# Reloading the context outputs of a first attention on another gate, and a margin in the plan ahead of the feed-forward's norm matmuls

## The chip, the cores and the metric

The kernel runs on one core of a Trainium2 chip. A core has a matrix engine (TensorE, PE in the profile, with its weight loads shown apart as PEld), a vector engine (VectorE, DVE), a scalar engine (ScalarE, ACT), GpSimd (POOL) and the engine that issues the transfers (SyncE, SP). Each works through its own list of instructions in a fixed order and waits for the others by semaphores. The metric is the device time of one execution in microseconds (us); what is given for a kernel is the median of several executions.

## The reference

A trunk of two layers over 1024 latent tokens and 256 context tokens, width 1024, 16 heads of 64. Layer 0 uses neighbourhood attention, layer 1 sliding-window attention; each layer ends with a gated feed-forward with a short convolution. The part that the change touches is the end of layer 0's attention and the start of its feed-forward:

```python
q, k, v = attn_inputs(h, w_in, gq, gk, n_kv)
q_c, k_c, v_c = attn_inputs(hc, w_in, gq, gk, n_kv, with_q=not last)
o = neighbourhood_attention(q, k, v, k_c, v_c, na_rpb[j])
x = x + gt1 * (o @ w_out)
o_c = attend(q_c, k_c, v_c, sink=sink).reshape(bsz, n_ctx, D_MODEL)
ctx = ctx + gt1c * (o_c @ w_out)
h = modulate(rmsnorm(x, g_ffn[i]), sh2, sc2)
x = x + gt2 * conv_ffn(h, ffn_w_up[i], ffn_conv_w[i], ffn_conv_b[i], ffn_w_down[i])
hc = modulate(rmsnorm(ctx, g_ffn[i]), sh2c, sc2c)
ctx = ctx + gt2c * conv_ffn(hc, ffn_w_up[i], ffn_conv_w[i], ffn_conv_b[i], ffn_w_down[i])
```

All of it is float32. The kernel makes a product of two float32 matrices out of three matrix multiplications of a reduced type: every operand is split into a high part and a low part, and hi·hi, lo·hi and hi·lo are added in PSUM. A split costs one ScalarE copy (the high part) and one subtraction on VectorE or GpSimd (the low part).

## The kernel before

Nothing in the program text fixes the order of the work. Each stage is described as operations with an engine, an estimated duration, tokens that are read and written, a key (a smaller key goes first among those that are ready) and places in rings of buffers; `class Sched` (L61) simulates the engines with these estimates and so settles the order in which each engine's instructions are issued. A wrapper records them, and so every row of the profile names L51, the wrapper's line; tiles are told apart by their names.

Layer 0's attention runs over 8 head pairs (0 to 7). For each, ten token tiles (8 of latents, numbers 8 and 9 of context) get their q, k and v by matmuls into `mm` tiles (`mm<-whi,h0hi` and the like); `s` are the scores, `S` the softmax tiles on VectorE and ScalarE, `pt` the transposes, `pthi`, `ptlo` the split probabilities, `pv` the products with v, and `osb` the output of a unit. The outputs of head pairs 0 to 6 are stored to `o_dram`; those of pair 7 stay on chip and are split directly.

Then comes the output projection, of class `Oproj` (L722), made as `op0` at L962 with three gates, lists of tokens on which operations wait. `gate` is the set of the qkv accumulations of all ten token tiles of head pair 7; `c_gate` is only those of the context tiles 8 and 9; `w_gate` is that of tile 4. Its methods:

- `weights` (L751) loads one 128x1024 slice of the output weights into a `woraw` tile of the ring `raw` (3 buffers), and splits it into `whi` (ScalarE) and `wlo` (GpSimd or VectorE in this stage, as the plan picks), in the ring `w` (4 pairs).
- `split` (L737) splits loaded attention outputs; for the context (`c == 2`) it waits on `c_gate`, for the latents on `gate`.
- `project` (L769) makes the matmuls of one output slice, waiting on `gate`.

`plan_oproj0` (L1184) plans the context part and the loads of the latent part. Two transfers bring the context outputs of head pairs 0 to 3 and 4 to 6 back as `craw` tiles (also in `raw`); they are split into `o2chi` and `o2clo`. Eight output slices (dt 0 to 7) follow, each 24 matmuls `mm<-o2chi,whi`, `mm<-o2clo,whi`, `mm<-o2chi,wlo` of 128x256, 192 in all. `evac` (L1197) loads the residual of a slice from `in_xseq_dram` into a `cx` tile (ring `qraw`, 2 buffers), adds the projected slice times its gate on VectorE and stores the sum to `c_dram`. The latent outputs come back as `oraw` tiles and are split into `o0hi`, `o0lo`, `o1hi`, `o1lo`.

All operations of this stage have keys from `OKEY` = 1000 up, so that the attention's operations go first where both are ready.

`ffn` (L1246) then plans the rest: the latent part of the output projection (`oacc<-o0hi,whi` and the like, 128x512; residual additions into `x` tiles), and, in `plan_ctx` (L1462), the context's norm. There `xc` is loaded from `c_dram`, `plan_sums` (L1289) squares it on ScalarE and adds the eight squares into `nsum` on VectorE, and `plan_bc` (L1313) sums over partitions on TensorE (`mp<-invd,nsum`), takes the root on VectorE and GpSimd (`n1v`, `n1y`, `n1t`) and broadcasts it (`bc`). A parameter `late` of `plan_bc` stands in the plan as an operation of its own engine, which does nothing on the chip, between the sums and the `mp` matmuls: the plan takes the sums to be there by so much later.

Of the kernel before, what the change touches and what calls it, by code (L numbers as in the profile page):

```python
# [19 lines left out]
KT = 8  # L20
# [16 lines left out]
WBUFS = 4  # L37
# [189 lines left out]
def trunk_kernel(ctx, tc, xperm, xseq, cc, wmod, bmod, gnorm, na_wqkv, na_gq, na_gk, na_bias, na_wo,  # L227
# [3 lines left out]
    act, dve, pool, pe, dma = [InOrder(tc, e) for e in (nc.scalar, nc.vector, nc.gpsimd, nc.tensor, nc.sync)]  # L231
# [103 lines left out]
    def t_dve(n):  # L335
        return 0.065 + n / 960.0
# [453 lines left out]
    with tc.tile_pool(name="x0", bufs=1, reuse_waits="tile") as xp, \  # L790
# [10 lines left out]
        for c, parts, key in ((2, 2, 0), (0, 4, 2), (1, 4, 30)):  # L801
            t0, n = CH[c]
# [21 lines left out]
        for v in range(2):  # L824
            J = {}
# [97 lines left out]
        for j in range(4):  # L923
# [5 lines left out]
                  key=50 + 2 * j, acq=[("w", ("w", j), 1)], rel=[("raw", j)])  # L929
            sa.op("dve", 0.87, lambda e, j=j: slabs.lo(j, e), reads=[("raw", j), ("wh", j)] + [("modc", 1)] * (j > 0),  # L930
                  writes=[("wl", j)], key=50 + 2 * j, rel=[("raw", j)])
# [25 lines left out]
    def pair(a):  # L957
# [3 lines left out]
    sc = Sched(dict(CAPS, klt=1))  # L961
    op0 = Oproj(sc, 0, 2, TC, psa, [("q0", HP - 1, tt, "acc") for tt in range(NT)],  # L962
                [("q0", HP - 1, tt, "acc") for tt in (8, 9)], [("q0", HP - 1, WG0, "acc")])
    OKEY = 1000
# [219 lines left out]
    def plan_oproj0():  # L1184
        C = {}
        for j, (a, b) in enumerate(((0, 4), (4, 7))):
            def load(e, j=j, a=a, b=b):
                C[j] = rpool.tile([P, 4, TC], F32, tag="raw", name="craw")
                dma.dma_start(C[j][:, :b - a], o_dram[0][a:b, :, T:].rearrange("k p t -> p k t"))
            sc.op("dma", 1.8, load, reads=[("od", k, 4) for k in range(a, b)] + op0.gate, writes=[("craw", j)], key=OKEY + j,  # L1190
                  acq=[("raw", ("craw", j), 2)])
            op0.split(2, (2, "j", j), 256 * (b - a), lambda j=j, n=b - a: C[j][:, :n], lambda x, a=a, b=b: x[:, a:b, :],
                      OKEY + j, [("craw", j)], [("craw", j)])
        parts = [[(x, 2, "j", int(k > 3)) for x in ("oh", "ol")] for k in range(7)] + [[(x, 2, 7) for x in ("oh", "ol")]]
        xin = {}

        def evac(dt, I):  # L1197
            def load(e):
                xin[dt] = wk.tile([P, 384], F32, tag="qraw", name="cx", bufs=2)
                dma.dma_start(xin[dt][:, :TC], xseq[:, KT * T + dt * TC:KT * T + (dt + 1) * TC])  # L1200
            xk = ("cx", dt)
            sc.op("dma", 0.6, load, reads=[("q0", HP - 1, ORDER[-1], "raw")], writes=[xk], key=OKEY + dt, acq=[("qraw", xk, 1)])

            def add(e):
                dve.scalar_tensor_tensor(out=xin[dt][:, :TC], in0=op0.acc[dt][:, :TC], scalar=modc[:, 0, 1, 2, dt:dt + 1],
                                         in1=xin[dt][:, :TC], op0=ALU.mult, op1=ALU.add)
            sc.op("dve", t_dve(TC), add, reads=[I, ("modc", 2), xk], writes=[xk], key=OKEY + dt, rel=[I], port=False)
            sc.op("dma", 0.6, lambda e: dma.dma_start(c_dram[:, dt * TC:(dt + 1) * TC], xin[dt][:, :TC]), reads=[xk],
                  writes=[("cd", dt)], key=OKEY + dt, rel=[xk])

        for dt in range(KT + NPRE):
            op0.weights(dt, na_wo[dt % KT], OKEY + dt, KT, [("craw", 0), ("craw", 1)] if dt >= WBUFS else ())
            if dt < KT:
                op0.project(dt, OKEY + dt, parts, evac)
        R = {}
        for kt in range(HP - 1):
            def load(e, kt=kt):
                R[kt] = rpool.tile([P, T], F32, tag="raw", name="oraw")
                dma.dma_start(R[kt], o_dram[0][kt, :, :T])
            r = ("oraw", kt)  # L1220
            sc.op("dma", 1.8, load, reads=[("od", kt, su) for su in range(4)] + op0.gate, writes=[r], key=OKEY + 0.5 + kt,
                  acq=[("raw", r, 4)])
            for c in range(2):
                op0.split(c, (c, kt), 512, lambda c=c, kt=kt: R[kt].rearrange("p (k r c) -> p r k c", k=8, r=16)[:, 8 * c:8 * c + 8],
                          lambda a, kt=kt: a[:, kt, :].rearrange("p (r k c) -> p r k c", r=8, k=8), OKEY + 0.5 + kt, [r], [r])
# [20 lines left out]
    def ffn(l, opj, xt1, todo):  # L1246
# [8 lines left out]
        sc = Sched(dict(b=8, raw=3, w=WBUFS, x=8, sr=SRB, g=GB, g2=GB, sq=2), {"b", "raw", "w", "x", "sr", "g", "g2", "sq"})  # L1255
# [57 lines left out]
        def plan_bc(nm, n, J, key, late=0.0):  # L1313

            I = (f"nm{nm}",)
            nt = n // P

            def mp(e):
                J["mp"] = bank("mp")
                for i in range(nt):  # L1320
                    pe.matmul(J["mp"][:, i:i + 1], J["t"][:, i * P:(i + 1) * P], invd, start=True, stop=True)

            sc.op(f"late{nm}", late, lambda e: None, reads=[I + ("sums",)], writes=[I + ("here",)], key=key)
            sc.op("pe", 0.11 * 2 * nt, mp, reads=[I + ("sums",), I + ("here",)], writes=[I + ("mp",)], key=key, acq=[("b", I + ("mp",), 1)])

            def v(e):
                for s in "vyt":
                    J["n" + s] = tiny.tile([P, 4], F32, tag="n1" + s, name="n1" + s, bufs=1)[:, :nt]
                dve.tensor_scalar(out=J["nv"], in0=J["mp"][:, :nt], scalar1=EPS, scalar2=None, op0=ALU.add)
            sc.op("dve", 0.07, v, reads=[I + ("mp",)], writes=[I + ("v",)], key=key, rel=[I + ("mp",)])  # L1330
            sc.op("pool", 0.96, lambda e: pool.tensor_tensor(out=J["ny"], in0=J["nv"], in1=mhalf[:, :nt], op=ALU.pow),
                  reads=[I + ("v",)], writes=[I + ("y",)], key=key)

            def newton(e):
                y, t, v = J["ny"], J["nt"], J["nv"]
                dve.tensor_tensor(out=t, in0=y, in1=y, op=ALU.mult)
                dve.scalar_tensor_tensor(out=t, in0=t, scalar=-0.5, in1=v, op0=ALU.mult, op1=ALU.mult)
                dve.scalar_tensor_tensor(out=y, in0=t, scalar=1.5, in1=y, op0=ALU.add, op1=ALU.mult)
            sc.op("dve", 0.473, newton, reads=[I + ("y",)], writes=[I + ("y",)], key=key)

            def dg(e):
                for i in range(nt):
                    dve.tensor_scalar(out=J["t"][:, 512 + i * P:512 + (i + 1) * P], in0=idf, scalar1=J["ny"][:, i:i + 1],
                                      scalar2=None, op0=ALU.mult)
            sc.op("dve", 0.15 * nt, dg, reads=[I + ("y",)], writes=[I + ("dg",)], key=key)

            def bc(e):
                J["bp"] = bank("bc")
                for i in range(nt):
                    pe.matmul(J["bp"][:, i * P:(i + 1) * P], ones, J["t"][:, 512 + i * P:512 + (i + 1) * P], start=True, stop=True)  # L1350
            sc.op("pe", 0.22 * nt, bc, reads=[I + ("dg",)], writes=[I + ("bp",)], key=key, acq=[("b", I + ("bp",), 1)])

            def bs(e):
                J["bc"] = J["t"][:, :n]
                act.activation(J["bc"], J["bp"][:, :n], AF.Copy)
            sc.op("act", t_actp(n), bs, reads=[I + ("bp",), I + ("mp",)], writes=[I + ("bc",)], key=key,
                  rel=[I + ("bp",), I])
# [104 lines left out]
        def plan_ctx():  # L1462
            n = TC
# [6 lines left out]
                dma.dma_start(Xc[0], c_dram.rearrange("p (k t) -> p k t", k=KT))  # L1470
            sc.op("dma", 3.6, load, writes=[("xc", k) for k in range(KT)], key=-30)
            J = plan_sums("c", n, xc, ct, lambda k: -20)
            plan_bc("c", n, J, -20)
            hc = []
            csh, csc = [modc[:, l, 1, v, :] for v in (3, 4)]
            for k in range(KT):
# [10 lines left out]
            for ft in range(FT):  # L1487
                key = KC + 8.7 * ft
                st = {}
                I = ("uc", ft)  # L1490
                for part in range(2):
                    W = cw(("cw", ft, part), w_up[l, ft + part * FT], key - 16 + 3 * part, 4)
                    for k0 in range(0, KT, 2):
                        def mm(e, part=part, k0=k0, W=W, st=st):
# [3 lines left out]
                            for k in (k0, k0 + 1):  # L1498
# [6 lines left out]
                              writes=[I, ("hcu",)], key=key + 3 * part, acq=[("b", I, 6)] if part == 0 and k0 == 0 else (), rel=[t])  # L1505
# [11 lines left out]
                for part in range(2):  # L1517
                    w = cv[:, l, ft + part * FT, :]
                    for tap, d in ((0, -1), (2, 1)):
# [8 lines left out]
                      reads=[g + (1,)], writes=[g + (0,)], key=key)  # L1528

                def ghi(e, st=st, ft=ft):  # L1530
# [4 lines left out]
                      reads=[g + (0,), g + ("h",)], writes=[g + ("l",)], key=key, rel=[("gt", ft)])  # L1535
                t = ("cd", ft)
                W = cw(t, w_down[l, ft], key - 8, KT)
                for dt in range(KT):
                    def mm(e, ft=ft, dt=dt, W=W):
# [4 lines left out]
                        for i, (w, b) in enumerate(((0, 0), (0, 1), (1, 0))):  # L1544
# [3 lines left out]
                          key=key + 13, acq=[("b", ("dnc", dt // 2), 2)] if ft == 0 and dt % 2 == 0 else (), rel=[t, g])  # L1548
            key = KU + 5
            for j in range(2):  # L1550
# [7 lines left out]
                for dt in range(4 * j, 4 * j + 4):  # L1558
                    def ev(e, dt=dt, R=R):
# [5 lines left out]
                      writes=[("c2", j)], key=key, rel=[r])  # L1565
# [20 lines left out]
        def t34_(i):  # L1586
            if not t34:
# [3 lines left out]
              writes=[("dsh",)], key=-50)  # L1591
        rx = lambda c, k, n=1: [("xt", c, k // 2)] * n if c or not last else []
        kb = 46.0 * n_todo
        for k in range(KT):
            key = 46.0 * (1 if not last else 0) + k
# [17 lines left out]
        for step in range(3):  # L1613
            for j in range(4):
                key = kb + (30.0 * j + 4 * step if not last else 2.0 * j + 8 * step)
                sh = shift[:, j + 4:j + 5]
                if step == 0:
# [3 lines left out]
                        writes=[("x", 0, j)], key=key)  # L1621
# [6 lines left out]
                else:  # L1628
                    sc.op("dve", tst, stt(1, j, 1, j + 4, dsh[:, j:j + 1], 1, j), reads=[("x", 1, j + 4), ("dsh",)],
                          writes=[("x", 1, j)], key=key, rel=rx(1, j + 4))  # L1630
# [8 lines left out]
        for j in range(4):  # L1639
            key = kb + (30.0 * j + 12 if not last else 2.0 * j + 24)  # L1640
            k = j + 4
# [472 lines left out]
    sc = Sched(CAPS)  # L2114
# [351 lines left out]
```

## Time and profile before

| What | Value |
|---|---|
| Median of 3 runs | 2849.25 us (2848.09 to 2849.77) |
| Profiled execution, its own time | 2851.74 us |
| Span of the profiled execution | 2850.0 us |
| Mean granted TensorE clock | 0.989 |
| VectorE busy | 2324.1 us (82%) |
| Transfers | 367.20 MB, 129 GB/s in the mean |

The span is cut into stages of quite different limits; the first attention ends near 720 us. Views by windows give the busy time of each engine in a stretch, in the order PE, PEld, DVE, ACT, POOL, then the granted clock (1.00 is full speed), the busy share of the transfer engines and GB/s. In a timeline, the brackets at the end of a row give the idle time of the engine ahead of it and what ended that. A matmul's duration in a row includes its way through the pipeline, so that successive rows overlap.

### The profile page before, as it was taken

Reading aid. Unit: us, or ns where it says so; the run is one execution under the profiler, and the core shown is the slowest. Engines: PE = TensorE matmul, PEld = TensorE weight load, DVE = VectorE, ACT = ScalarE, POOL = GpSimd, SP = SyncE. Lnnn points to the kernel's source line nnn. Section 1 sums busy time; section 2 is a strip of 40 time slices with the busy share of each in tenths; the row PEclk is TensorE's granted clock in tenths of the full one; section 3 lists DMA queues with packets and bytes.
Section 4 is the critical chain, followed back from the end, with each engine's and each line's share of the span. In section 5 each row is a group of like instructions: output and inputs, shape, how many; then the busy total and the mean of one; then the engine's idle time right before and its main releaser. Section 6 shows DMA issues by size and latency. Waiting matters only on the chain.

```text
span 2850.0 us, 46124 instructions
## 1 busy us (share of the span) xinstructions
PE 2784.4 (98%) x16344; PEld 2455.3 (86%) x16344; DVE 2324.1 (82%) x5243; ACT 1713.2 (60%) x3382; POOL 400.1 (14%) x675
## 2 busy tenths in 40 slices
PE   6999999999999999999999999999999999999999
PEld 5999999998789987777788888999987788888887
DVE  7888888888688687877797787999987988888757
ACT  5877777778456554444454457888873554455443
POOL 1222212223000000000010006455520000000000
PEclk9999999999999999999999999999999999999999
DMA  6222222314745544444375551010234323324745
GB/s 247 65 95 80 83 67 75 96 60 125 250 142 192 183 162 140 154 142 160 135 258 194 181 169 29 13 34 16 73 128 138 116 105 111 111 93 149 253 148 182
DMA packets 140953, 367.20 MB, mean 129 GB/s; under 512 B 21425, under 2 KB 34225, under 8 KB 139313
## 3 DMA queue, kind: packets, MB, share of 16 engines
q1 hardware_dynamic: 140720, 364.25, 38.1%
q8 instruction: 129, 2.11, 0.3%
q14 instruction: 104, 0.84, 0.1%
HBM read 297.21 MB, written 66.98 MB: 128 GB/s over the span
## 4 chain that ended last, share of the span: by engine, by line
PE 69%; DVE 4%; ACT 2%; issue 1%; DMA 1%; DVEq 0%; ACTq 0%; SPq 0%
PE ua L51 17%; PE dn L51 15%; PE uc L51 13%; PE mm L51 6%; PE oacc L51 4%; PE ud L51 4%; PE pt L51 3%; PE pv L51 2%; PE dnc L51 2%; PE s L51 2%; DVE S L51 1%; PE mod L51 1%; ACT S L51 1%; DVE ptlo L51 1%; DVE x L51 0%
## 5 line engine op out<-in xcount | busy, mean ns | idle before, releaser
L51 ACT ACTIVATE whi<-wraw 128x512 fp32r<-128x512 f32 (+1 forms) x264 | 212.6, 806 | 203.6 <-PE uc L51 62.7
L51 DVE TENSOR_TENSOR wlo<-wraw,whi 128x512 fp32r<-128x512 f32 (+1 forms) x264 | 239.2, 907 | 45.3 <-ACT whi L51 44.8
L51 DVE TENSOR_TENSOR ptlo<-pt,pthi 128x512 fp32r<-128x512 f32 (+2 forms) x384 | 223.2, 595 | 48.6 <-ACT pthi L51 45.0
L51 PE MATMUL dn<-ghi,wlo 128*128 128x512 f32 x616 | 242.4, 394 | 0.0
L51 PE MATMUL dn<-ghi,whi 128*128 128x512 f32 x616 | 242.4, 394 | 0.0
L51 PE MATMUL dn<-glo,whi 128*128 128x512 f32 x616 | 242.3, 393 | 0.0
L51 ACT ACTIVATE pthi<-pt 128x512 fp32r<-128x512 f32 (+2 forms) x384 | 195.1, 524 | 71.1 <-PE pt L51 61.1
L51 ACT ACTIVATE S<-S,m 128x640 f32<-128x640 f32 (+3 forms) x288 | 220.8, 768 | 22.7 <-DVE m L51 19.6
L51 DVE SCALAR_TENSOR_TENSOR u<-c,cv,u 128x1023 f32<-128x1023 f32 x176 | 223.2, 1279 | 6.8 <-ACT u L51 5.8
L51 ACT ACTIVATE whi<-s 128x1024 fp32r<-128x1024 f32 (+1 forms) x120 | 113.3, 945 | 191.4 <-PE uc L51 137.4
L51 ACT ACTIVATE ghi<-graw 128x512 fp32r<-128x512 f32 x154 | 96.4, 631 | 190.2 <-PE dn L51 108.4
L51 PE MATMUL pt<-idr,S 128*128 128x128 f32 x1280 | 199.2, 278 | 6.8 <-DVE sm L51 2.6
L51 PE MATMUL mm<-whi,h0hi 128*128 128x384 f32 x512 | 181.1, 354 | 0.4 <-ACT qraw L51 0.4
L51 DVE TENSOR_TENSOR glo<-graw,ghi 128x512 fp32r<-128x512 f32 x154 | 105.4, 688 | 83.8 <-ACT ghi L51 76.4
L51 PE MATMUL mm<-wlo,h0hi 128*128 128x384 f32 x512 | 172.3, 337 | 0.0
L51 PEld LDWEIGHTS pt<-idr,S 128*128 128x128 f32 x1280 | 153.5, 143 | 17.4 <-DVE ptlo L51 3.9
L51 DVE TENSOR_TENSOR wlo<-s,whi 128x1024 fp32r<-128x1024 f32 (+1 forms) x120 | 129.6, 1080 | 40.6 <-ACT whi L51 40.5
L51 POOL TENSOR_TENSOR qy<-qv,mhalf 128x4 f32<-128x4 f32 (+2 forms) x120 | 126.2, 1052 | 227.0 <-DVE qv L51 197.0
L51 PE MATMUL pv<-ptlo,v 128*128 128x256 f32 (+1 forms) x688 | 153.9, 297 | 1.2 <-DVE ptlo L51 1.2
L51 PE MATMUL pv<-pthi,v 128*128 128x256 f32 (+1 forms) x688 | 147.7, 287 | 4.1 <-DVE osb L51 3.0
L51 PE MATMUL ua<-t12hi,whi 128*128 128x512 f32 x352 | 138.7, 394 | 5.5 <-ACT t12hi L51 3.9
L51 POOL TENSOR_TENSOR n1y<-n1v,mhalf 128x4 f32<-128x4 f32 (+1 forms) x9 | 9.2, 1025 | 953.3 <-DVE n1v L51 950.7
(315 smaller groups left out, 8906.4 us busy)
## 6 DMA issues: line engine op xcount, KB each, us to landing
wraw<-in_w_up_dram SPq DMA_DIRECT2D x132, 512.0 KB, 3.4
wm<-in_wmod_dram SPq DMA_DIRECT2D x80, 512.0 KB, 4.0
wraw<-in_w_down_dram SPq DMA_DIRECT2D x44, 512.0 KB, 3.5
graw<-g_dram SPq DMA_DIRECT2D x44, 512.0 KB, 4.4
wraw<-in_w_down_dram SPq DMA_DIRECT2D x88, 256.0 KB, 3.0
graw<-g_dram SPq DMA_DIRECT2D x66, 256.0 KB, 2.8
slab<-in_na_wqkv_dram SPq DMA_DIRECT2D x32, 384.0 KB, 3.7
woraw<-in_na_wo_dram SPq DMA_DIRECT2D x24, 512.0 KB, 4.4
```

Source lines behind the costliest of these rows:

```text
L51: r = f(*a, **k)
```

## The change

```diff
-            sc.op("dma", 1.8, load, reads=[("od", k, 4) for k in range(a, b)] + op0.gate, writes=[("craw", j)], key=OKEY + j,
+            sc.op("dma", 1.8, load, reads=[("od", k, 4) for k in range(a, b)] + op0.c_gate, writes=[("craw", j)], key=1000 + j,
                   acq=[("raw", ("craw", j), 2)])
             op0.split(2, (2, "j", j), 256 * (b - a), lambda j=j, n=b - a: C[j][:, :n], lambda x, a=a, b=b: x[:, a:b, :],
-                      OKEY + j, [("craw", j)], [("craw", j)])
+                      1000 + j, [("craw", j)], [("craw", j)])
...
         for dt in range(KT + NPRE):
-            op0.weights(dt, na_wo[dt % KT], OKEY + dt, KT, [("craw", 0), ("craw", 1)] if dt >= WBUFS else ())
+            op0.weights(dt, na_wo[dt % KT], 1000 + dt if dt < 4 else OKEY + dt, KT, [("craw", 0), ("craw", 1)] if dt >= WBUFS else ())
...
             J = plan_sums("c", n, xc, ct, lambda k: -20)
-            plan_bc("c", n, J, -20)
+            plan_bc("c", n, J, -20, 5.0)
```

Two edits have an effect. The load of the two `craw` tiles waits for the context tiles' accumulations of head pair 7 instead of for all ten tiles'. And the plan takes the context norm's sums to be ready 5.0 us later than before. Since `OKEY` is 1000, the keys written as 1000 are the same numbers as before. No operation is added or taken away; the plan gives another order.

On SP, whose list of transfers is in one order for all, the `craw` loads stood between the loads of the output weights, the residuals and the latent outputs:

```order
L51 DMA woraw<-in_na_wo_dram 128x1024
L51 DMA craw<-o_dram_75 128x4x256
L51 DMA cx<-in_xseq_dram 128x256
L51 DMA oraw<-o_dram_75 128x1024
L51 DMA craw<-o_dram_75 128x3x256
L51 DMA cx<-in_xseq_dram 128x256
```

Now both stand next to each other, further ahead in the list, within head pair 7:

```order
L51 DMA o_dram_75<-osb 128x256
L51 DMA craw<-o_dram_75 128x4x256
L51 DMA craw<-o_dram_75 128x3x256
L51 DMA bias<-in_na_bias_dram 128x640
L51 DMA o_dram_75<-osb 128x256
```

They moved ahead of every load of output weights; a load of position bias and an output store stand behind them.

On TensorE, at the end of the attention, the first context projection matmul stood behind the transposes of the first softmax tile after the last qkv matmuls (`kkc`, `klc`, `kkl`, `kll` are the keys' high and low parts, `st` and `idr` the operands of the transposes):

```order
L51 MATMUL pv<-pthi,v 128x256 x2
L51 MATMUL pt<-idr,st 128x128 x4
L51 MATMUL pv<-ptlo,v 128x256 x2
L51 MATMUL pv<-pthi,v 128x256 x2
L51 MATMUL pv<-ptlo,v 128x256 x2
L51 MATMUL pt<-idr,S 128x128
L51 MATMUL s<-kkc,q 128x256
L51 MATMUL s<-klc,q 128x256
```

The same place now:

```order
L51 MATMUL pv<-pthi,v 128x256 x2
L51 MATMUL mm<-o2chi,whi 128x256
L51 MATMUL mm<-o2clo,whi 128x256
L51 MATMUL mm<-o2chi,wlo 128x256
L51 MATMUL mm<-o2chi,whi 128x256
L51 MATMUL mm<-o2clo,whi 128x256
L51 MATMUL mm<-o2chi,wlo 128x256
L51 MATMUL mm<-o2chi,whi 128x256
L51 MATMUL mm<-o2clo,whi 128x256
L51 MATMUL mm<-o2chi,wlo 128x256
L51 MATMUL mm<-o2chi,whi 128x256
L51 MATMUL mm<-o2clo,whi 128x256
```

Twelve context projection matmuls went ahead of `pt<-idr,st`; six more follow `pt<-idr,S`, 27 the `s` and `pv` of the next rows, and so on. Behind the attention's last `pv` there are 36 of the 192 left, where there were 78. The other matmuls of this stretch are the same in number.

On TensorE, around the `mp` matmuls of the context norm, before (the number at the end of a name tells the tiles of one name apart):

```order
L51 MATMUL oacc_11137<-o0hi0_10374,whi_11079 128x512
L51 MATMUL oacc_11137<-o0lo0_10378,whi_11079 128x512
L51 MATMUL oacc_11137<-o0hi0_10374,wlo_11080 128x512
L51 MATMUL mp_11194<-invd_93,nsum_11141 128x1 x2
L51 MATMUL oacc_11198<-o0hi0_10374,whi_11086 128x512
L51 MATMUL oacc_11198<-o0lo0_10375,whi_11086 128x512
```

and now:

```order
L51 MATMUL oacc_11194<-o0hi0_10349,whi_11084 128x512
L51 MATMUL oacc_11194<-o0lo0_10353,whi_11084 128x512
L51 MATMUL oacc_11194<-o0hi0_10349,wlo_11085 128x512
L51 MATMUL mp_11230<-invd_93,nsum_11141 128x1 x2
L51 MATMUL oacc_11194<-o0hi0_10349,whi_11084 128x512
L51 MATMUL oacc_11194<-o0lo0_10353,whi_11084 128x512
L51 MATMUL oacc_11194<-o0hi0_10349,wlo_11085 128x512
L51 MATMUL oacc_11239<-o0hi0_10349,whi_11208 128x512
L51 MATMUL oacc_11239<-o0lo0_10350,whi_11208 128x512
L51 MATMUL oacc_11239<-o0hi0_10349,wlo_11209 128x512
```

Before, 48 `oacc` matmuls stood ahead of `mp` and the first one behind it began a new output slice; now 69 stand ahead, and three matmuls behind `mp` a slice begins with weights `whi_11208` and `wlo_11209`, of which `wlo_11209` is first used in the sixth matmul behind `mp`. From the norm's broadcast on, TensorE's order is the same in both.

VectorE's rows there follow suit. Before:

```order
L51 TENSOR_TENSOR nsum<-nsum,sq 128x256 x5
L51 TENSOR_SCALAR x_11127<-oacc,modc,x_11127 128x512
L51 TENSOR_SCALAR n1v<-mp 128x2
L51 TENSOR_TENSOR nsum<-nsum,sq 128x512
L51 TENSOR_TENSOR n1t<-n1y 128x2
```

and now:

```order
L51 TENSOR_TENSOR nsum<-nsum,sq 128x256 x5
L51 TENSOR_SCALAR x_11127<-oacc,modc,x_11127 128x512
L51 TENSOR_TENSOR nsum<-nsum,sq 128x512
L51 TENSOR_TENSOR wlo<-woraw,whi 128x1024 x2
L51 TENSOR_SCALAR n1v<-mp 128x2
L51 TENSOR_SCALAR x_11135<-oacc,modc,x_11135 128x512
```

Two weight splits moved from behind the norm's short operations to between the last sum and `n1v`.

## The prediction, made before the changed kernel ran

> **What bounds the kernel now.** I read first the page's busy shares, then busy time by windows around the end of the first attention (600 to 750 us), then TensorE's timeline there, then the chain of waits.
>
> ```profile
> PE 2784.4 (98%) x16344; PEld 2455.3 (86%) x16344; DVE 2324.1 (82%) x5243; ACT 1713.2 (60%) x3382; POOL 400.1 (14%) x675
> ...
> core 0: us, PE busy (x) PEld busy (x) DVE busy (x) ACT busy (x) POOL busy (x), PEclk, DMA share, GB/s
> 600.00:640.00 40.00, 40.00 (x296) 39.65 (x295) 32.12 (x114) 29.05 (x77) 7.43 (x11) 1.00 0.16 50
> 665.00:679.00 14.00, 8.91 (x53) 7.29 (x53) 13.76 (x43) 13.28 (x32) 6.92 (x7) 0.82 0.53 159
> 679.00:690.00 11.00, 11.00 (x76) 11.00 (x76) 8.12 (x23) 6.73 (x16) 4.95 (x5) 0.76 0.47 148
> 690.00:700.00 10.00, 9.07 (x76) 8.78 (x75) 9.60 (x28) 6.98 (x19) 3.61 (x3) 1.00 0.34 110
> 700.00:710.00 10.00, 10.00 (x85) 9.89 (x85) 9.41 (x29) 9.90 (x22) 1.29 (x1) 1.00 0.65 198
> 710.00:720.00 10.00, 9.06 (x75) 8.69 (x75) 8.89 (x15) 5.57 (x12) 1.33 (x1) 1.00 0.66 209
> 730.00:740.00 10.00, 7.04 (x32) 5.49 (x30) 4.45 (x9) 3.83 (x10) 0.00 (x0) 1.00 0.82 315
> 740.00:750.00 10.00, 9.63 (x39) 7.93 (x40) 6.57 (x15) 3.87 (x6) 0.70 (x1) 0.83 0.95 345
> ```
>
> TensorE is busy 98% of the span, so only its idle stretches and its slow clock can be won. It is full to 665 us. From 665 to 679 it idles 14 − 8.91 = 5.09 us while VectorE is busy 13.76 of 14: VectorE sets the pace there. The granted clock then stands at 0.76 over 11 us: 11 × 0.24 = 2.64 us lost. The second hole ends at the norm's sums:
>
> ```profile
> 669.12 0.51 PE L51 MATMUL pt<-idr,st 128*128 128x128 f32 x4 [1.26 <-POOL v L51]
> ...
> 675.23 0.45 PE L51 MATMUL pt<-idr,S 128*128 128x128 f32 x1 [2.65 <-DVE sm L51]
> ...
> 678.51 0.79 PE L51 MATMUL pv<-pthi,v 128*128 128x256 f32 x2 [0.88 <-ACT pthi L51]
> 679.11 0.41 PE L51 MATMUL mm<-o2chi,whi 128*128 128x256 f32 x1
> ...
> 715.86 0.22 PE L51 MATMUL pv<-ptlo,v 128*128 128x128 f32 x1
> 725.92 0.40 PE L51 MATMUL oacc<-o0hi,whi 128*128 128x512 f32 x1
> 740.37 0.61 PE L51 MATMUL mp<-invd,nsum 128*128 128x1 f32 x4 [3.33 <-DVE nsum L51]
> ...
> 716.08 3.65 PE mm L51 x30
> 720.27 3.70 DMA c_dram<-cx
> 723.98 4.07 DMA cx<-in_xseq_dram
> 728.68 1.88 DMA c_dram<-cx
> 730.69 4.78 DMA xc<-c_dram
> 740.97 7.20 PE oacc L51 x24
> 748.62 31.30 PE oacc L51 x138
> ```
>
> The first context projection matmul stands behind the waits of 665 to 679 us. After the attention's last matmul (716.08) the chain is the leftover projection, a store, a residual load, a store, the reload of the context stream, and the sums; TensorE waits 3.33 us for them in front of `mp`.
>
> **The change part by part.**
>
> *T0, loads and splits earlier: 0.* Both `craw` loads move far up in SP's order, ahead of a bias load and an output store of head pair 7; the four splits follow them.
>
> ```profile
> L51 ACT ACTIVATE o2chi<-craw x2: 833/948/1062, 670.5 to 676.7; 128x1024 fp32r<-128x1024 f32 x1, 128x768 fp32r<-128x768 f32 x1
> L51 DVE TENSOR_TENSOR o2clo<-craw,o2chi x2: 946/1078/1210, 677.6 to 681.2; 128x1024 fp32r<-128x1024 f32 x1, 128x768 fp32r<-128x768 f32 x1
> ...
> DMA to landing us min/median/max: 3.5/3.8/4.1
> ```
>
> They bring ScalarE 1.06 + 0.83 and VectorE 1.21 + 0.95 us into a stretch where TensorE is full (40.00 of 40) and the two are busy 29.05 and 32.12: hidden there. Without that cover they would cost VectorE's 2.2. Behind the loads SP holds only bias and output stores; a late bias would be held by at most one landing, 4.1 us, and this stretch has 7.9 us of VectorE slack. I take 0.
>
> *T1, projection matmuls into the holes: −5.1.* In the changed order 36 context-projection matmuls are left behind the attention's last one, where 78 were: 42 move ahead. One costs 3.65/30 = 0.122 us, so 42 × 0.122 = 5.1 us leave the path. They need room, and 5.09 idle plus 2.64 of slow clock give 7.7. The new first ones stand ahead of the rows that end the waits of 1.26 and 2.65, so TensorE does not rest and the clock should not fall. If they merely displaced work, the term is 0; with the room wholly used, −7.7.
>
> *T2, the attention's end itself: −1.5.* VectorE paces it. Its busy time in the windows of 665 to 720 is 13.76 + 8.12 + 9.60 + 9.41 + 8.89 = 49.78 of 55, so at most 5.2 us can go. By rows, its work up to the last `osb` is about unchanged: two `o2clo` leave, two `cx` additions and small splits come. Of its idle time 11 − 8.12 = 2.9 lies in 679 to 690, where TensorE ran at 0.76; I give back half of that, −1.5. The ends: −5.2, and +4.8 if two weight splits that now go to GpSimd hold VectorE:
>
> ```profile
> 669.31 2.38 POOL L51 TENSOR_TENSOR wlo<-woraw,whi 128x1024 fp32r<-128x1024 f32 x1 [0.20 <-ACT whi L51]
> ...
> 695.20 1.67 POOL L51 TENSOR_TENSOR o1lo<-oraw,o1hi 128x512 fp32r<-128x512 f32 x1 [2.80 <-ACT o1hi L51]
> ...
> 710.38 1.33 POOL L51 TENSOR_TENSOR o0lo<-oraw,o0hi 128x512 fp32r<-128x512 f32 x1 [1.26 <-ACT o0hi L51]
> ...
> 675.74 0.28 DVE L51 TENSOR_TENSOR o0lo<-osb,o0hi 128x128 fp32r<-128x128 f32 x1
> 695.65 1.37 DVE L51 TENSOR_TENSOR o0lo<-osb,o0hi 128x128 fp32r<-128x128 f32 x1
> 710.48 2.31 DVE L51 TENSOR_TENSOR wlo<-woraw,whi 128x1024 fp32r<-128x1024 f32 x1
> 715.79 1.22 DVE L51 TENSOR_TENSOR wlo<-woraw,whi 128x1024 fp32r<-128x1024 f32 x1 [0.28 <-ACT whi L51]
> ```
>
> A VectorE split took 1.37 instead of 0.28, and 2.31 instead of 1.22, each while a GpSimd split ran: both times it ended only after GpSimd's did (696.87, 711.71). So a GpSimd split costs VectorE between 0 and its own 2.38; the two rows say 1.1 each.
>
> [...]
>
> *T3, the wait at `mp` and the clock after it: −5.1.* The 5.0 in the plan puts `mp` behind 69 oacc matmuls instead of 48. The wait, 3.33 us, goes. After it 24 oacc took 7.20 us, 0.300 each, against 31.30/138 = 0.227 later: 24 × 0.073 = 1.75 us of slow clock (0.83 in 740 to 750). 3.33 + 1.75 = 5.1. Is the chain early enough? I count from the attention's last matmul, E:
>
> ```profile
> 717.04 0.42 DVE L51 TENSOR_TENSOR osb<-pv,pvup 64x256 f32<-64x256 f32 x1
> ...
> L51 DVE SCALAR_TENSOR_TENSOR cx<-mm,modc,cx x8: 465/479/486, 693.6 to 728.2; 128x256 f32<-128x256 f32 x8
> ...
> 737.78 2.53 DVE L51 TENSOR_TENSOR nsum<-nsum,sq 128x256 f32<-128x256 f32 x5
> 740.23 0.74 DVE L51 SCALAR_TENSOR_TENSOR x<-oacc,modc,x 128x512 f32<-128x512 f32 x1
> ...
> 741.61 1.99 ACT L51 ACTIVATE whi<-woraw 128x1024 fp32r<-128x1024 f32 x2
> ...
> 742.81 1.23 DVE L51 TENSOR_TENSOR wlo<-woraw,whi 128x1024 fp32r<-128x1024 f32 x1
> ```
>
> The last `osb` ends 1.4 after E; the sixth `cx` addition stands right behind it and ends at E + 1.9 to 2.9; SP then issues its store and the last load (4.07): E + 7.4; its addition, E + 7.9; from there to the last sum it is 740.31 − 728.68 = 11.6 (store, reload, squares): E + 19.5. TensorE reaches `mp` after 36 × 0.122 + 69 × 0.227 = 20.1. Ahead by 0.6: the wait is gone, though barely. Bounds: 0 saved, or 5.1.
>
> *T4, what is late next: +1.6.* Behind the sums VectorE and ScalarE have two weight splits still to make, and only five oacc (1.1 us) stand between `mp` and the first that needs a `wlo` of them. Before, the split that followed the sums ended at 742.81 + 1.23 = 744.04, 3.7 after the last sum; with the three short norm operations behind it now, 3.3. So the weights are there at E + 22.8, TensorE wants them at E + 20.1 + 1.1 = 21.2: a new wait of 1.6 us (bounds 0, and 3.3 if TensorE is earlier). It lies amid full work; the trace shows 1.26 us of wait at 669 alone without slow matmuls behind it, so I add no clock.
>
> Sum: 0 − 5.1 − 1.5 − 5.1 + 1.6 = −10.1 on 2851.74 of the profiled execution, thus 2841.7; the median of the runs shown lies 2.5 lower, 2849.25, so **2839**. Its own range from T1, T2 and T4: 2836 to 2842.
>
> [...]
>
> **The rivals.** 0.2% (5.7 us: under 2843.6, over 2855.0) is what a measurement of this kernel can tell from no change.
>
> R1, `mp` still waits. The margin of E + 19.5 against 20.1 is thin; a load at 5 instead of 4.07, or two splits ahead of the addition (2 × 1.23), put the chain 3 us back: 2.4 of wait return, with 1.75 of clock, and T4 is up to 2.2 instead of 1.6. 2839 + 2.4 + 0.6 + 1.75 = 2843.8. Chance 0.15.
>
> R2, GpSimd's two splits hold VectorE where it paces the attention: 2 × 1.1 to 2 × 2.38, mid 3.5: 2842.5. For it, the two long rows; against, VectorE had gaps in 679 to 690. Chance 0.16.
>
> R3, more is won: VectorE's waits go with the clock (T2 −4) and the splits come in time (T4 0): 2839 − 2.5 − 1.6 = 2835. Chance 0.12.
>
> R4, the other side: residual loads hold VectorE. Six `cx` additions, not four, now stand in VectorE's order ahead of the last `osb`, each behind a load that waits for a store: 3.70 + 4.07 = 7.8 us a round, two buffers, so 3.9 per addition where nothing else fills it. Three such waits cost 11.7 in front of the softmax work and another slow-clock stretch, 2.64; T2's gain is lost: 2839 + 11.7 + 2.6 + 1.5 = 2854.8, and slower than before from 3.3 us per wait on, judged against the 10.1 won. Against it: the additions before 716 us waited for nothing that the views show. Chance 0.08, of which 0.05 lands above 2855.
>
> That the order does not move is excluded by the rows of the order; that the moved matmuls only displace the wait (T1 = 0, the rest as summed) gives 2844: 0.05.
>
> **How the numbers follow.** Forecast 0.44, R3 0.12, R2 0.16, R1 0.15, T1 void 0.05, R4 0.08. Faster: all of the forecast and R3 (0.56), most of R2 (0.13) and under half of R1 (0.06), 0.75; slower 0.05 of R4 and 0.01 of R1, 0.06; the same, the rest, 0.19. The range runs from R3's 2835, a little below, to past R1: 2834 to 2846.
>
> **What would show it.** Right: `mm<-o2chi` starting near 668, TensorE busy nearly 14 of 14 in 665 to 679 and clock 1.00 to 690; the first oacc near 718.5 instead of 725.92; no `nsum` wait at `mp`, and a new wait of 1 to 2 us of oacc for `wlo`. Wrong: VectorE waiting for `cx<-in_xseq_dram` ahead of an `osb` (R4), split rows over 2 us beside GpSimd (R2), `mp` behind `nsum` still (R1). If the first oacc starts after 722, T1 fails, and with it most of the forecast.

## The result and the profile after

| Kernel | Median | Range | Ratio to before |
|---|---|---|---|
| before | 2849.77 us | 2848.09 to 2850.26, 5 runs | |
| changed | 2839.17 us | 2834.91 to 2841.56, 5 runs | 0.9957 (0.9945 to 0.9969) |

The change makes the kernel 10.6 us faster, 0.43% (0.31 to 0.55%). The forecast was 2839. The profiled execution of the changed kernel took 2841.56 us with a span of 2839.7, 10.3 less than the span before.

Both profiles can be cut at three marks on TensorE that exist in either order: the last qkv matmul of head pair 7, the first `oacc` and the first `uc` of the feed-forward. Between them lie the two stages that the change touches. One view by windows for each stage and kernel (first the length, then busy time of PE, PEld, DVE, ACT and POOL, the clock, the transfers); the kernel before:

```profile
665.00:725.92 60.92, 53.61 (x402) 51.01 (x401) 53.11 (x138) 44.58 (x98) 18.09 (x15) 0.92 0.55 171
...
725.92:821.00 95.08, 91.75 (x410) 75.73 (x409) 62.64 (x101) 39.35 (x59) 1.71 (x2) 0.98 0.59 208
```

and the changed kernel:

```profile
666.00:718.51 52.51, 49.36 (x403) 47.91 (x401) 48.99 (x137) 44.67 (x97) 23.44 (x15) 1.00 0.60 191
...
718.51:809.20 90.69, 90.43 (x410) 74.63 (x409) 61.96 (x100) 38.58 (x58) 1.71 (x2) 1.00 0.60 212
```

Length less PE's busy time is PE's idle time; since the matmuls are the same, I put a difference in busy time down to the clock, which was granted at 0.92 and then 1.00 in the first stage, at 0.98 and then 1.00 in the second. The first stage (A) lost 8.41 us: 7.31 − 3.15 = 4.16 of idle time and 53.61 − 49.36 = 4.25 of slow clock. The second (B) lost 4.39: 3.33 − 0.26 = 3.07 idle and 91.75 − 90.43 = 1.32 slow clock. That is 12.8 in all.

The same stretches as before the change, by windows of the changed kernel, and TensorE's rows at the places that the prediction named:

```profile
PE 2780.0 (98%) x16344; PEld 2451.8 (86%) x16344; DVE 2324.2 (82%) x5244; ACT 1714.2 (60%) x3381; POOL 404.7 (14%) x675
...
665.00:679.00 14.00, 13.34 (x107) 13.08 (x107) 13.90 (x44) 12.49 (x29) 7.24 (x6) 1.00 0.55 171
679.00:690.00 11.00, 10.99 (x92) 10.71 (x92) 10.93 (x33) 9.85 (x22) 4.74 (x3) 1.00 0.71 215
730.00:740.00 10.00, 9.86 (x45) 7.57 (x43) 7.72 (x17) 4.43 (x8) 0.70 (x1) 1.00 0.94 346
...
668.74 0.28 PE L51 MATMUL mm<-o2chi,whi 128*128 128x256 f32 x1
...
714.04 0.27 PE L51 MATMUL pv<-ptlo,v 128*128 128x128 f32 x1
718.51 0.40 PE L51 MATMUL oacc<-o0hi,whi 128*128 128x512 f32 x1
734.18 0.50 PE L51 MATMUL mp<-invd,nsum 128*128 128x1 f32 x4
740.12 0.71 PE L51 MATMUL bc<-nsum,ones 128*128 128x128 f32 x4 [0.17 <-DVE nsum L51]
```

The context projection starts at 668.74, TensorE is busy 13.34 of 14 and the clock stays at 1.00. `mp` has no bracket: it waited for nothing. VectorE and the transfers of the chain, then:

```profile
716.00 0.42 DVE L51 TENSOR_TENSOR osb<-pv,pvup 64x256 f32<-64x256 f32 x1
729.85 2.54 DVE L51 TENSOR_TENSOR nsum<-nsum,sq 128x256 f32<-128x256 f32 x5
734.76 2.36 DVE L51 TENSOR_TENSOR wlo<-woraw,whi 128x1024 fp32r<-128x1024 f32 x2 [0.25 <-ACT whi L51]
...
717.38 2.67 DMA cx<-in_xseq_dram
720.69 1.88 DMA c_dram<-cx
722.64 4.87 DMA xc<-c_dram
```

The last sum is there at 729.85 + 2.54 = 732.39, 1.8 ahead of `mp`. The two weight splits behind it end near 736.0 and 737.1. The sixth matmul behind `mp`, the first that needs one of them, waits for it; its row on the weight-load side of TensorE is:

```profile
736.04 0.19 PEld L51 LDWEIGHTS oacc<-o0hi,wlo 128*128 128x128 f32 x1 [0.52 <-DVE wlo L51]
```

It starts 0.48 after the matmul ahead of it, where its neighbours start 0.23 apart: a wait of 0.25 us.

### The profile page after: what moved, and what is told of

It reads as the page before. It is cut to its first block, busy times and chain, and to the rows that moved or that the text cites. A ratio compares the mean times of both kernels' runs of the same rounds, so it can differ in the third digit from the quotient of the medians.

```text
span 2839.7 us, 46113 instructions
## 1 busy us (share of the span) xinstructions
PE 2780.0 (98%) x16344; PEld 2451.8 (86%) x16344; DVE 2324.2 (82%) x5244; ACT 1714.2 (60%) x3381; POOL 404.7 (14%) x675
## 4 chain that ended last, share of the span: by engine, by line
PE 68%; DVE 5%; ACT 2%; issue 1%; DMA 0%; POOL 0%; DVEq 0%; SPq 0%; ACTq 0%
PE ua L51 17%; PE dn L51 15%; PE uc L51 13%; PE mm L51 6%; PE ud L51 4%; PE oacc L51 4%; PE pt L51 3%; PE pv L51 2%; PE dnc L51 2%; PE s L51 2%; DVE S L51 1%; PE mod L51 1%; DVE ptlo L51 1%; ACT S L51 1%; DVE x L51 0%
```

## The experiments

Each was timed against the kernel before on the same chip, and three chips were used in all, so medians of different runs are best compared by their ratios. In the texts on record, E is the end of the attention's last `pv` matmul.

**The changed kernel again**, without an edit.

> The changed kernel once more, beside its parts on one chip. Theory (additive: the gate brings about 6 us, the margin about 5): 2839, within 2836 to 2842. Rival (chance of one chip): 2844 or more. The first oacc is expected 8 to 9 us earlier, counted from the attention's last qkv matmul, than in the kernel before.

2837.16 us (2835.48 to 2841.47), ratio 0.9960 (0.9948 to 0.9972). Stage A took 52.50, stage B 91.20 us.

**The gate alone.**

```diff
-            plan_bc("c", n, J, -20, 5.0)
+            plan_bc("c", n, J, -20)
```

> The gate without the margin: mp stands behind 48 oacc again. Theory: first oacc as early as in the changed kernel (8 us earlier than before), then mp waits about 3.0 us for nsum (the chain's last sum at E + 18.1, TensorE at E + 4.2 + 48 x 0.227 = E + 15.1) and the clock drops behind it (1.75): 4.8 us are lost against the changed kernel, 2844. Rival (the margin does nothing of its own, the shorter chain has removed the wait): 2839, no nsum wait at mp.

2841.04 us (2840.15 to 2843.73), ratio 0.9970 (0.9959 to 0.9981). By windows, the two stages, and TensorE's row at `mp`:

```profile
666.10:718.60 52.50, 49.35 (x403) 47.90 (x402) 49.05 (x137) 44.66 (x97) 23.45 (x15) 1.00 0.60 192
718.60:813.20 94.60, 91.75 (x411) 75.87 (x410) 61.88 (x100) 38.30 (x59) 1.70 (x2) 0.98 0.58 203
...
732.51 0.60 PE L51 MATMUL mp<-invd,nsum 128*128 128x1 f32 x4 [2.85 <-DVE nsum L51]
```

Stage A is that of the changed kernel to the hundredth, stage B that of the kernel before: a wait of 2.85 (3.0 expected) and busy time 1.32 longer than in the changed kernel. So the margin is worth 94.60 − 90.69 = 3.9 us beside the gate; the medians, on one chip, differ by as much (2841.04 against 2837.16). The median came out 3 below the expected 2844; the stages agree with the theory in kind, with 3.9 us lost where it had 4.8, and the rival (no wait at `mp`) falls.

**The margin alone**: the kernel before with the 5.0.

```diff
-            plan_bc("c", n, J, -20)
+            plan_bc("c", n, J, -20, 5.0)
```

> The margin without the gate: mp behind 69 oacc, the attention as before. Theory: the wait of 3.33 and the slow clock of 1.75 go, a wait of up to 0.5 for the weights' low parts may come: 2849.8 - 4.6 = 2845. Rival (the wait only moves, to bc or to the oacc behind mp): 2849 to 2850, with a new PE wait of 3 us or more in 725 to 750.

2846.01 us (2843.95 to 2848.72), ratio 0.9986 (0.9977 to 0.9994).

```profile
665.00:726.30 61.30, 54.06 (x403) 51.27 (x401) 52.48 (x138) 44.62 (x98) 17.98 (x15) 0.92 0.57 174
...
726.30:816.80 90.50, 90.16 (x408) 74.74 (x409) 63.22 (x101) 39.65 (x59) 1.70 (x2) 1.00 0.60 216
```

Now it is the other way round: stage A as before, stage B 4.6 us shorter. The wait did not move elsewhere: only 90.50 − 90.16 = 0.34 us of idle time is left in stage B. The two parts add up: 0.30% and 0.14% against 0.40 to 0.43% together.

**The loads and splits alone.** The context projection is held back in the plan, so that its first matmul stands behind the waits again.

```diff
+        sc.op("hold", 11.0, lambda e: None, reads=op0.gate, writes=[("cgo",)], key=0)
...
+        parts[0].append(("cgo",))
```

> The changed kernel with the loads and splits as early as in it, but the context projection held back in the plan by 11 us behind the last qkv accumulation, so that its first matmul stands behind the waits again, about where it stood before (15 of its matmuls are left behind the last pv). Theory (the matmuls in the holes carry the gain, the early splits nothing): idle 4 to 5 us and a slow clock return in the 15 us behind the last qkv matmul; the first oacc comes 58 to 60 us after the last qkv matmul instead of 52.5, and the median is 2842 to 2845. Rival (the early loads and splits relieve VectorE, and that carries it): 54 or less, 2837 to 2840.

2844.09 us (2841.44 to 2845.51), ratio 0.9974 (0.9963 to 0.9985).

```profile
664.50:721.70 57.20, 51.76 (x402) 49.89 (x401) 51.85 (x135) 44.21 (x95) 18.96 (x16) 0.94 0.54 177
...
674.71 0.48 PE L51 MATMUL pt<-idr,S 128*128 128x128 f32 x1 [2.78 <-ACT S L51]
```

The wait (2.78, where 2.65 stood before) and the slow clock (51.76 − 49.36 = 2.4 us) are back with the matmuls' place, and 57.20 − 52.51 = 4.7 of stage A's gain of 8.4 are gone. The stage is 0.8 shorter than expected, and 3.7 us of the gain remain, half of it idle time (7.31 less 57.20 − 51.76 = 5.44) and half slow clock (53.61 − 51.76 = 1.85). This order leaves 15 matmuls behind the attention's last `pv`, not 78, so matmuls still moved ahead of it, into later waits; whether that or the early splits keeps the 3.7 was not taken apart. The median lies in the theory's range and off the rival's.

**A larger margin**: 8.0, `mp` behind 84 oacc.

> The changed kernel with a margin of 8.0 in place of 5.0: mp behind 84 oacc instead of 69. Theory (with 5.0 the sums are in 1.8 us ahead of mp, so nothing is left to win): the same as the changed kernel within 1 us, about 2838, from the last qkv matmul to the first uc 143 to 144 us. Rival (a thin margin still costs; more is better): 141 to 142. Rival the other way (the norm's later work runs into the weights' splits): over 145.

2837.04 us (2833.58 to 2838.72), ratio 0.9953 (0.9941 to 0.9966): no difference from 5.0 that could be told. Stage B took 90.70, as with 5.0. Stage A, which this edit cannot touch, took 53.50, and so the first `uc` came after 144.2, a little outside the expectation. That 1.0 us is a measure of how much one execution of the same order differs from another.

**Four buffers for the residuals.**

```diff
-                xin[dt] = wk.tile([P, 384], F32, tag="qraw", name="cx", bufs=2)
+                xin[dt] = (wk.tile([P, 4, DH], F32, tag="qn", name="cx", bufs=2).rearrange("p h d -> p (h d)") if dt % 2
+                           else wk.tile([P, 384], F32, tag="qraw", name="cx", bufs=2))
...
-            sc.op("dma", 0.6, load, reads=[("q0", HP - 1, ORDER[-1], "raw")], writes=[xk], key=OKEY + dt, acq=[("qraw", xk, 1)])
+            sc.op("dma", 0.6, load, reads=[("q0", HP - 1, ORDER[-1], "raw")], writes=[xk], key=OKEY + dt, acq=[("qn" if dt % 2 else "qraw", xk, 1)])
```

> The changed kernel with four buffers for the residual tiles cx instead of two (odd columns in the ring qn): the plan then leaves no context matmul behind the attention's last pv, instead of 36. Theory (TensorE's work is conserved; what can go is its idle time up to the attention's end, 3.1 us): 1 to 2.5 us faster than the changed kernel, 2835.5 to 2837, first uc 141 to 142.5 after the last qkv matmul. Rival (the six cx additions wait for stores and loads and hold VectorE): VectorE's waits for cx loads, now 0.8 in all, were the price, and 4 us go. Rival (the attention's end moves back by all that stood behind it): no change.

2847.75 us (2843.77 to 2850.42), ratio 0.9992 (0.9984 to 1.0001): nearly the whole gain is lost, against every one of the three expectations. Stage A takes 61.2 us, stage B 90.9 as in the changed kernel. The chain of waits shows where (start, duration, what):

```profile
687.62 4.51 DMA oraw<-o_dram
692.16 0.87 ACT o0hi L51 x2
693.03 0.72 ACT o1hi L51 x2
693.75 0.51 ACT st L51 x2
694.33 0.68 POOL st L51
695.06 1.25 PE pt L51 x8
...
695.06 0.75 PE L51 MATMUL pt<-idr,st 128*128 128x128 f32 x4 [6.52 <-POOL st L51]
...
690.00:700.00 10.00, 4.94 (x26) 4.94 (x27) 7.64 (x15) 6.81 (x14) 0.67 (x1) 0.52 0.79 258
```

In this order one load of latent outputs is issued only at 687.62 and lands at 692.1; ScalarE's splits of it stand in its order ahead of `st`, which the attention needs, and TensorE waits 6.52 us; the clock in 690 to 700 is 0.52. The mechanism is that of R4 (an engine held in its order by a late load, with the attention's work behind it), but on ScalarE and by `oraw`, where R4 had VectorE and `cx`: VectorE's waits for `cx` were 0.7 us.

**The same without the margin.**

> The four cx buffers without the margin: mp behind 48 oacc. Theory (the shorter chain also brings TensorE to mp sooner): mp waits 2.5 to 3.5 us again and the clock drops behind it; 3 to 4 us slower than the four buffers with the margin. Rival (two buffers, a store and a load behind each other, made the chain late): mp waits under 1 us, as fast as with the margin.

2845.67 us (2842.24 to 2849.98), ratio 0.9985 (0.9976 to 0.9994), no slower than with the margin, as the rival had it; stage A takes 60.4 us, again long. The theory's wait did not come. With no context matmul behind the end, the last residual addition comes ahead of it:

```profile
724.59 0.48 DVE L51 SCALAR_TENSOR_TENSOR cx<-mm,modc,cx 128x256 f32<-128x256 f32 x1 [0.39 <-PE mm L51]
735.11 2.53 DVE L51 TENSOR_TENSOR nsum<-nsum,sq 128x256 f32<-128x256 f32 x5
...
727.24 0.33 PE L51 MATMUL pv<-ptlo,v 128*128 128x128 f32 x1
738.37 0.50 PE L51 MATMUL mp<-invd,nsum 128*128 128x1 f32 x4
```

The sums are ready at 737.64, `mp` starts at 738.37. So the margin is worth 3.9 us beside the gate, where 36 matmuls stand between the attention's end and the last addition, and nothing here, where none does.

**All weight splits of the stage on VectorE.**

```diff
+    op0.w_engs = ("dve",), (1.13,)
```

> The changed kernel with the weight splits of this stage on VectorE alone (three splits of 1.22 leave GpSimd; the plan then leaves 57 context matmuls behind the attention's last pv, not 36). [...]

2841.20 us (2839.49 to 2847.32), ratio 0.9975 (0.9964 to 0.9985). The attention's last `pv` ends 46.1 us after the last qkv matmul, 2.2 earlier than in the changed kernel (48.31), but 57 matmuls and two waits for the weights (1.68 and 0.76 us) follow, and stage A takes 57.30, 4.8 longer than in the changed kernel. The run changes two things at once, the engine and the order, and so does not say what the splits on GpSimd cost VectorE by themselves.

**The idea carried to the second attention**, on top of the changed kernel: its latent outputs of the first 512 tokens are loaded and split once the first four latent tiles have their qkv.

```diff
+    op1.gate0 = [("q1", NKV - 1, tt, "acc") for tt in range(4)]
...
-            g = self.c_gate if c == 2 else self.gate
+            g = self.c_gate if c == 2 else self.gate0 if c == 0 and self.gate0 else self.gate
...
-                for k in (2,) if c == 2 else (0, 1):
+                for k in (2,) if c == 2 else (0, 1) if self.gate0 is None else (c,):
...
-                sc.op("dma", 1.0, load, reads=[("od", kt, c)] + op1.gate, writes=[r], key=key, acq=[("raw", r, 2)])
+                sc.op("dma", 1.0, load, reads=[("od", kt, c)] + (op1.gate if c else op1.gate0), writes=[r], key=key, acq=[("raw", r, 2)])
```

> The same idea carried to the second attention, on top of the changed kernel: its latent outputs of the first 512 tokens are loaded back and split once the qkv accumulations of the first four latent tiles are done, not all ten; in the order 63 of the 192 projection matmuls are left behind the last pv, where there were 99. Theory (moved matmuls fill the waits of 2050 to 2070 us and keep the clock up): 36 x 0.237 = 8.5 at most, room 3.96 idle + 5.1 of slow clock; 4 to 8 us faster than the changed kernel, 2831 to 2835. Rival (only the shape of the first attention allowed it; here they displace work): 2838 or more.

2831.47 us (2827.66 to 2837.27), ratio 0.9939 (0.9925 to 0.9953): the lowest median of this study, in the theory's range. The interval of the ratio still touches that of the changed kernel in its second run (0.9948 to 0.9972), so the stage itself has to show the gain. From the last qkv matmul of the second attention to the first `oacc<-o1hi` behind its projection, first the changed kernel in its second run, then this one:

```profile
2043.94:2131.73 87.79, 83.07 (x475) 71.95 (x474) 73.44 (x199) 60.60 (x125) 26.61 (x41) 0.96 0.47 157
```

```profile
2042.26:2125.43 83.17, 81.88 (x491) 70.66 (x490) 75.16 (x202) 61.21 (x128) 25.02 (x41) 1.00 0.41 146
```

The stage is 4.6 us shorter. TensorE's idle time falls from 87.79 − 83.07 = 4.72 to 83.17 − 81.88 = 1.29, and the slow clock is gone (0.96, now 1.00), just as in the first attention (0.92, then 1.00).

## Why the prediction was right, and where it was off

The forecast, 2839, met the median of 2839.17, and the mechanism of T1 and T3 is what the profile shows. That the number fits to a fifth of a microsecond is luck: the two stages gave 12.8 us where the sum had 10.1, and what they gave too much was lost again in places that the change does not touch. The five executions of the changed kernel alone spread over 6.7 us.

- **T0 (0)** holds. Up to the last qkv matmul the changed profile runs 1.0 us later (666.0 against 665.0), but its output stores already stood 0.7 later at 386 us, long before the moved loads, and in the experiments with the early loads this matmul starts at 664.5 to 667.1. The splits are gone from the tail of VectorE, but other work took their place there (see T2).
- **T1 (−5.1)** measured −5.6: from the last `pv`'s end to the first oacc 716.08 to 725.92 was 9.84, and 714.31 to 718.51 is now 4.20. That the matmuls' place matters is shown by the run with the loads alone: the wait and the slow clock return with the place, at a price of 4.7.
- **T2 (−1.5)** was right in its mechanism and the term most undersized. By windows from the last qkv matmul to the end of the last `osb`, before and now:

```profile
665.00:717.46 52.46, 45.50 (x336) 43.10 (x336) 48.03 (x129) 40.80 (x92) 18.09 (x15) 0.90 0.51 156
```

```profile
666.00:716.42 50.42, 47.27 (x385) 45.82 (x384) 47.75 (x133) 43.10 (x94) 23.44 (x15) 1.00 0.59 188
```

VectorE's work is unchanged, 48.03 and 47.75, as I had it; its idle time fell from 4.43 to 2.67, by 1.8. So the last `osb` ends 2.0 earlier, counted from the last qkv matmul; the last `pv`, behind which VectorE now finishes two weight splits before it turns to that `osb`, 2.8 (48.31 instead of 51.08). With T1, stage A was predicted at −6.6 and gave −8.4. The room was larger than the 7.7 I had in T1. I priced the slow clock only in 679 to 690 (2.64), but 665 to 679 stood at 0.82 too, which on 8.91 us of work is another 1.6 (8.91 × 0.18); together that is 4.2, as against the 4.25 measured. The means hide what the clock did. Narrower windows of the kernel before:

```profile
674.00:675.00 1.00, 0.00 (x0) 0.00 (x0) 0.96 (x3) 1.00 (x3) 0.00 (x0) 0.50 0.40 138
...
679.00:684.00 5.00, 5.00 (x28) 5.00 (x28) 3.14 (x5) 1.29 (x4) 1.73 (x2) 0.50 0.65 184
685.00:690.00 5.00, 5.00 (x42) 5.00 (x41) 4.93 (x18) 4.98 (x11) 3.22 (x3) 1.00 0.20 66
```

The clock was at 0.50 from 674 on, while TensorE still sat in the wait of 2.65 us that had begun at 672.6, and back at 1.00 by 685.
- **T3 (−5.1) and T4 (+1.6)**, −3.5 together, measured −4.4. The wait of 3.33 and the slow clock went, as shown by the margin alone and the gate alone (−4.6 and −3.9 in stage B). In the terms of the sum that is 3.33 of wait and 1.32 of slow clock (I had 1.75), less T4. T4's wait came, but as 0.25 us instead of 1.6. The last `cx` load took 2.67 instead of the 4.07 I carried over, so that the sums stood at E + 18.1, not 19.5. The first weight split ended 3.6 after them, close to the 3.3 I had, at E + 21.7, and TensorE wanted it at E + 21.5. The working was right and its input a single row of a quantity that varies (the `cx` loads' landing, 1.9 to 5.0).
- **The rest.** Stages A and B together gave 12.8, the spans differ by 10.3. Of the 2.5 given back, 1.0 lies ahead of the last qkv matmul, and the second attention's qkv stage, unchanged in its order, took 2.1 more; 0.6 came back elsewhere. One view of the tile `mm` for each (minimum, median and maximum in ns, the first and the last start in us):

```profile
L51 PE MATMUL mm<-wlo,h1hi x256: 333/337/522, 1689.2 to 2057.4; 128*128 128x384 f32 x128
```

```profile
L51 PE MATMUL mm<-wlo,h1hi x256: 332/337/522, 1677.3 to 2047.6; 128*128 128x384 f32 x128
```

From its first to its last such matmul that is 368.2 before and 370.3 in the changed kernel, but 366.1 in the changed kernel's second run: no effect of the change.

Of the rivals, R1 (`mp` still waits) did not come; the gate alone shows the wait that the margin removes. Long rows of the kind that R2 names are there, but no dearer than before: beside GpSimd's work two VectorE rows are long again, `qv` with 1.21 and one `S` with 1.50, where others of their kind take 0.15 and 0.55: 2.0 too much together, as against 2.2 before (the rows stand at the end). Both stand beside latent splits on GpSimd, neither beside one of the two weight splits that moved there, which start at 688.74 and 704.42. R3's larger gain was there in part: stage A gained 1.8 more than the sum had, and T4's wait nearly vanished. R4's kind of hold did not occur in the changed kernel, where VectorE waited 0.8 us in all for `cx` (1.3 in its second run), but four buffers called it up on another engine. The moved matmuls did not merely displace the wait, or stage A would not have become 8.4 us shorter.

## What to carry to other kernels

A reload that waits for more than it needs leaves matmuls unusable in the very holes where they would cost nothing; look for the narrowest gate, and price a filled hole as idle time plus the slow clock over the whole stage around it (here 4.2 and 4.3 us). Where a plan sets the order, a wait can be removed by telling the plan that its operand is later than it thinks, and here more margin than needed (8.0 for 5.0) cost nothing that could be told. The margin is worth something only where the engine really comes too early: with four buffers it was worth nothing. More buffers are no gain of their own: here they gave another order, in which one late load held ScalarE ahead of work that TensorE waited for, 6.5 us long.

## What the runs showed of the hardware

Some rows of VectorE and GpSimd that ran at the same time took longer than others of their kind, now on one engine and now on the other, all in the changed kernel. A split of 128x1024 on GpSimd took 2.41 us where no weight split on VectorE met it. The one at 704.42 took 3.91: VectorE's `S` of 128x640 had begun 0.01 before it and a weight split followed at once, and VectorE's two took their usual 0.54 and 1.21, so here it was GpSimd's row that grew. Likewise a split of 128x512 on GpSimd took 1.74 instead of 1.28 to 1.30 where it began 0.09 after a split on VectorE. The other way round, `qv` and `S` took 1.21 and 1.50 on VectorE where they began 0.11 and 0.12 after a split on GpSimd. The rows:

```profile
670.35 2.41 POOL L51 TENSOR_TENSOR wlo<-woraw,whi 128x1024 fp32r<-128x1024 f32 x1 [0.19 <-ACT whi L51]
704.42 3.91 POOL L51 TENSOR_TENSOR wlo<-woraw,whi 128x1024 fp32r<-128x1024 f32 x1 [3.54 <-ACT whi L51]
...
704.41 0.54 DVE L51 TENSOR_SCALAR S<-S,sm 128x640 f32<-128x640 f32 x1
704.88 1.21 DVE L51 TENSOR_TENSOR wlo<-woraw,whi 128x1024 fp32r<-128x1024 f32 x1
...
682.41 0.69 DVE L51 TENSOR_TENSOR o1lo<-oraw,o1hi 128x512 fp32r<-128x512 f32 x1
682.50 1.74 POOL L51 TENSOR_TENSOR o0lo<-oraw,o0hi 128x512 fp32r<-128x512 f32 x1 [7.38 <-ACT o0hi L51]
...
672.71 1.30 POOL L51 TENSOR_TENSOR o1lo<-oraw,o1hi 128x512 fp32r<-128x512 f32 x1
695.38 1.28 POOL L51 TENSOR_TENSOR o1lo<-oraw,o1hi 128x512 fp32r<-128x512 f32 x1 [2.79 <-ACT o1hi L51]
...
672.82 1.21 DVE L51 TENSOR_SCALAR qv<-qv 128x4 f32<-128x4 f32 x1
695.50 1.50 DVE L51 TENSOR_SCALAR S<-S,sm 128x640 f32<-128x640 f32 x1
...
691.25 0.42 DVE L51 TENSOR_TENSOR ptlo<-pt,pthi 128x256 fp32r<-128x256 f32 x1
691.29 1.29 POOL L51 TENSOR_TENSOR o0lo<-oraw,o0hi 128x512 fp32r<-128x512 f32 x1
```

Each of the long rows above is the one that started second, and the two long VectorE rows end after GpSimd's (674.03 after 674.01, 697.00 after 696.66). Starting second was not enough by itself: at 691.29 a split of 128x512 on GpSimd began 0.04 after one of 128x256 on VectorE and took 1.29. What makes a row long these runs do not show. Of the row at 704.42 even the order is unsure: its lead of 0.01 us proves little, since the profile calls spans on GpSimd rough.
